# The out-projection of a hybrid layer in halves of 512 columns, and the step that frees the next input's memory by itself

## The chip, the cores and the metric

The kernel runs on 1 core of a Trainium2 chip. The metric is the device time of one execution in microseconds (us). The engines are named as in the profile: PE (TensorE matmuls) with PEld (its weight loads), DVE (VectorE), ACT (ScalarE), POOL (GpSimd) and SP (SyncE, which issues the DMAs here).

## What is computed

Two layers of a mixer on 1024 latent tokens and 256 context tokens of width 1024, in float32. Each layer normalises its input, modulates it, and projects it at once to the inputs of three branches: a convolution, windowed attention (8 heads, windows of 128 tokens, with the context as extra keys) and a gated linear attention (GLA). Every branch is gated; the three lie side by side as 1024 columns and go through one out-projection, whose result is scaled by a gate and added to the input:

```python
y_l = jnp.concatenate([a_l, b_l, c_l], axis=-1) @ w_out      # [1024, 1024] @ [1024, 1024]
xl = xl + gate[:, None] * y_l
if update_ctx:                                               # first layer alone
    y_c = jnp.concatenate([a_c, b_c, c_c], axis=-1) @ w_out  # [256, 1024] @ [1024, 1024]
    xc = xc + mod_c[2 * D:] * y_c
...
return _rms_norm(xl) * final_norm_w
```

## The kernel before

Tokens are worked in 10 tiles of 128: tiles 0 and 1 are the context, 2 to 9 the latent tokens. The second layer needs no out-projection of the context, so there are 10 + 8 = 18 tiles to project out. All matrix products are made in three passes: each operand is split into hi + lo (a cast to the narrower type `F32R`, and the difference), and `three` (L670) adds hi x hi, hi x lo and lo x hi over 8 k-tiles of 128 rows.

*What sets the order.* The program is written as generators ("lanes"). Each yields conditions (a buffer is free, a flag is set, a tile is written). `loop` (L201) runs them against a small model of the engines' clocks at build time: of the lanes whose condition holds, the one with the lowest priority number issues its next instructions. The engines then run their instructions strictly in that order. The model counts a matmul of 256 columns as 107 ns and one of 512 as 213 ns, so a change in one lane can move instructions of all others. Out-projection tiles have priority 8 and more, the in-projection and the layer's main lane (`program`, `phase_a`, `phase_bc`) 9, attention 1 to 2.

*Memory.* WS0 and WS1 hold one group of 256 weight columns each, hi and lo (4096 columns a partition). WR0 to WR2 hold raw pieces from memory (512 columns). SM0 to SM14 are small tiles. H1, H2_0, H2_1 and HC hold the modulated input as hi and lo; attention and the out-projection reuse them later: HC for keys and queries, H1 for values, probabilities and the hi half of a token tile. In the profile the numbers of buffers are left out: H is H1, H2_0 or H2_1, ps a PSUM bank.

*The in-projection's end and attention.* The last two groups of the in-projection (6 and 7, attention's gates) take turns by token chunks, and attention starts among them. Group 6 gives back its WS slot after its last chunk, group 7 after its own, which is the last of all; the flag `h2out` then says that H2_0 and H2_1 are free.

*The out-projection's weights* are loaded by `loader` (L650) in four quarters of 256 columns: o0 in a WS slot, o1 in H2_0 after `h2out`, o2 in a WS slot, o3 in H2_1. A quarter comes in four pieces of two k-tiles (256 KB, 2 KB a partition), each a DMA to a WR slot and a split: a cast on ACT or DVE and a subtraction on DVE or POOL.

*The out-projection of a tile* (`out_tiles`, L1465) waits for both attention units of the tile, splits the tile's 1024 columns of the mixed branches into hi and lo, and multiplies: the token tile is the stationary side, the weights move. `out_mm` (L1442) does a quarter, 24 matmuls of 256 columns; two quarters fill a PSUM bank of 512 columns. Two lanes take the even and the odd tiles. The last two tiles hold two banks at once and do quarters 0 and 2 first. `x_old` (L1513) loads the old x to a WR slot between two quarters, `out_tail` (L1519) multiplies by the gate, adds the old x, sums the squares and stores the tile for the next layer.

*The end of a layer.* `phase_bc` (L1627) waits for all attention units and for the flags `ml` of both lanes, then frees two pieces of memory and sets `hfree..1` (the next input's tiles 2 to 5 may be written); then it waits for the whole out-projection and sets the flags for the other tiles. It does so in the main lane, of priority 9.

Of the kernel before, what the change touches and what calls it, by code (L numbers as in the profile page):

```python
# [34 lines left out]
class Engine:  # L35
    """an engine whose instructions are also put on the model's clock"""
# [12 lines left out]
class Model:  # L49
    """Estimate of when each engine is free and when each part of a tile was last written and read.  # L50
    It only decides the order in which instructions are issued; what has to wait for what is up to Tile."""
# [9 lines left out]
    def part(self, ap):  # L61
        """the times of ap's tile (written, read, written as seen by PE) and the pieces of it that ap covers"""
# [94 lines left out]
class Lane:  # L157
    """a generator of stages: what it yields says when its next stage may be issued"""
# [6 lines left out]
class Hybrid:  # L165
# [10 lines left out]
    # ---------------------------------------------------------------- issue order  # L176
# [6 lines left out]
    def when(self, c, lane):  # L183
        """the time from which condition c holds, None if that is not known yet"""
# [16 lines left out]
    def loop(self, last):  # L201
        """issues stages until lane `last` is done: of those that may start by now, the first by priority"""
# [33 lines left out]
    # ---------------------------------------------------------------- memory  # L236
    def memory(self):
# [13 lines left out]
        # a PSUM tile is used by one engine at a time, so there is one a bank, but for two of two banks  # L251
# [18 lines left out]
    def choice(self, cls, wide):  # L270
        """the free slots; those for wide tiles are left to these while self.rsv"""
        s = [x for x in self.slots[cls] if x[1] != self.kept]
        if cls == "SM" and (wide or self.rsv):
            s = [x for x in s if (x[1] in self.narrow) != wide]
        return s
# [14 lines left out]
    def mix_new(self, dt):  # L290
        """the upper half of mix anew, to hold what it doesn't hold yet"""
        t, old = self.tile("mix4", 4 * TC, dt), self.mixes[1]
        m, b = self.nc.part(t)
        m[1, b] = self.nc.touched(old) if old is not None else 0.0
        self.mixes[1] = t
        return t

    def mix(self, a, t, p=slice(None)):
        """tokens t of mix a, or of several that lie in the same half of mix"""
# [6 lines left out]
    def bank_of(self, cls, pair):  # L306
        """the bank that class cls would get"""
# [35 lines left out]
    def at(self, ap):  # L343
        """condition: all that has been issued has written ap"""
        return lambda: self.nc.written(ap)

    def rest(self, ap):
        """condition: nothing issued uses ap any more"""
        return lambda: self.nc.touched(ap)

    def sm_spare(self, cols):
        """like sm(), from the spare place if that is free"""
        return self.get("SF")[:, 0:cols] if self.slots["SF"] else self.sm(cols)

    # engines that can do the same work: the one that is done first
    def pick(self, *opts):
        """opts: (engine, estimated cost, function)"""
# [4 lines left out]
    def split(self, hi, lo, src):  # L362
        """hi + lo = src exactly, both float32r; src in SBUF"""
# [6 lines left out]
    def copy(self, o, a):  # L370
        """from PSUM"""
# [11 lines left out]
    def scale(self, o, a, s, f=1.0):  # L383
        """o = a * s * f; s one value a partition"""
# [6 lines left out]
    def square(self, junk, a, o):  # L391
        """o = sum of a * a"""
# [6 lines left out]
    # ---------------------------------------------------------------- set-up  # L399
# [37 lines left out]
    def rope_free(self):  # L437
        """between its uses the memory of the rotary table is one more small tile"""
# [3 lines left out]
    def rope_load(self):  # L442
        """generator: the rotary table again"""
# [24 lines left out]
    # ---------------------------------------------------------------- modulation  # L468
    def mod_add(self, l, b0, mt):
        """blocks b0 .. of the modulation from PSUM [128, blocks, 2], with their bias"""  # L470
# [9 lines left out]
    def mod_group(self, l, b0, n, raw):  # L480
        """generator: n blocks of 128 columns of the modulation, four k-tiles at a time in the column groups of the PE array;
        raw: the k-tiles of w_mod, loaded here if None"""
# [32 lines left out]
    # ---------------------------------------------------------------- h  # L515
    def hslot(self, i):
        """chunk and column offset of token tile i in the T-layout h"""
# [6 lines left out]
    def views(self):  # L524
        """the memory of h, free for it once the first weights have gone through"""
# [14 lines left out]
    def rstd(self, ss, scale, n):  # L540
        """(ss * scale + eps) ** -0.5 on [128, n]"""
# [13 lines left out]
    def part_h(self, l, i, k0, n, x):  # L555
        """generator: k-tiles k0 .. k0 + n - 1 of h for token tile i, from its normalised [128, 128 n] piece x"""
# [36 lines left out]
    def first_x(self, i, xt):  # L593
        """generator: token tile i of the input, loaded to xt and normalised there"""
# [16 lines left out]
    # ---------------------------------------------------------------- weights  # L611
# [14 lines left out]
    def load_w(self, key, src, ap, tile=None):  # L626
        """256 weight columns, split into hi and lo; ap(hl, k): k-tiles k and k + 1"""
        w = self.new_w(key, ap, tile)
        for k in range(0, 8, 2):
            self.go(self.piece(w, src, k), 3)  # L630

# [18 lines left out]
    def loader(self):  # L650
        """generator: all weights in the order of their use"""
# [6 lines left out]
        for l in range(2):  # L658
# [4 lines left out]
            yield from ws((l, "o0"), I["w_out"][l, 0])  # L663
            yield f"h2out{l}"
            self.load_w((l, "o1"), I["w_out"][l, 1], self.ws_ap(self.H2[0]))
            yield from ws((l, "o2"), I["w_out"][l, 2])
            self.load_w((l, "o3"), I["w_out"][l, 3], self.ws_ap(self.H2[1]))

    # ---------------------------------------------------------------- in-projection
    def three(self, out, st, mv, k0, k1):  # L670
        """out += st(hi,lo)^T mv(hi,lo) over k-tiles k0 .. k1 - 1 of 8, three float32r passes"""
# [7 lines left out]
    def t_group(self, l, g, ev, ctx_blocks, order=(1, 2, 0), lat_blocks=(0, 1), after=None, last=True):  # L679
        """T layout: ev(block, psum [128, n], t0, n, chunk)"""  # L680
# [1150 lines left out]
```

## Time and profile before

| | |
|---|---|
| time, median of 3 runs | 1357.74 us (1356.18, 1357.74, 1364.62) |
| span of the profiled execution, first to last instruction | 1357.4 us |
| PE busy | 1268.0 us, 93% of the span |
| PEld busy | 1084.6 us, 80% |
| DVE busy | 951.0 us, 70% |
| ACT busy | 558.6 us, 41% |
| POOL busy | 543.8 us, 40% |
| granted TensorE clock, mean | 0.983 |

The profile shows one execution; its own time is known as its span, 0.3 us under the median of the runs. A row of instructions gives their operation, the tiles written and read, the shape and the count. For a matmul the moving side comes first: `ps<-WS,H` moves weights in WS past a token tile in H. A matmul's duration is its way through the array, and several are under way at a time. Nearly all instructions carry the line of one helper (L43), so they are told apart by their tiles. Windows give busy us of an engine in a stretch, with the instructions' count.

### The profile page before, as it was taken

The page shows a single profiled execution, that of the slowest core. Times are in us where ns is not written, and L with a number is a line of the kernel's source. Part 1 is how long each engine was busy: PE and PEld are TensorE (multiplying, and loading weights), DVE is VectorE, ACT ScalarE, POOL GpSimd, SP SyncE. Part 2 cuts the span into 40 slices and gives each one's busy share as a digit, 9 for nine tenths or more (in the row PEclk, how much of TensorE's full clock was granted, in tenths as well). Part 3 has the DMA queues.
Part 4 walks back from the last instruction along what each step waited for, and adds up shares of the span by engine and source line. Part 5 has one row for each costly group of instructions (what it writes and reads, how often), then busy time and mean ns, then how long its engine had stood idle before and what let it go on. Part 6 is the DMA issues. An engine that isn't in the chain of part 4 may idle for free.

```text
span 1357.4 us, 24183 instructions
## 1 busy us (share of the span) xinstructions
PE 1268.0 (93%) x9070; PEld 1084.6 (80%) x9070; DVE 951.0 (70%) x1852; ACT 558.6 (41%) x1239; POOL 543.8 (40%) x769
## 2 busy tenths in 40 slices
PE   6999986898999999999999989988899999999997
PEld 3667976787788676887998978977797888898997
DVE  5844895789655366875666686896957478887864
ACT  3720351121223364665663451251113156776751
POOL 1410046766222233464353032046783244645530
PEclk9999997899999999999999999989999999999999
DMA  9353112321212433343113452113322113311112
GB/s 331 137 147 97 55 32 58 83 79 44 67 32 65 131 118 89 104 129 97 42 55 98 132 191 62 55 37 78 97 57 77 34 48 101 98 44 51 62 37 78
DMA packets 105045, 116.46 MB, mean 86 GB/s; under 512 B 38464, under 2 KB 65376, under 8 KB 104928
## 3 DMA queue, kind: packets, MB, share of 16 engines
q1 hardware_dynamic: 104928, 114.92, 28.4%
q8 instruction: 71, 1.16, 0.3%
q14 instruction: 46, 0.38, 0.1%
HBM read 95.47 MB, written 19.42 MB: 85 GB/s over the span
## 4 chain that ended last, share of the span: by engine, by line
PE 49%; DVE 10%; POOL 8%; issue 5%; DMA 4%; ACT 2%; SPq 0%; POOLq 0%; DVEq 0%; ACTq 0%
PE ps L43 49%; DVE SM L43 5%; POOL SM L43 5%; DVE H L43 2%; DMA WR<-in_w_in_dram 2%; POOL WR L43 2%; DVE WS L43 1%; DVE mix L43 1%; ACT SM L43 1%; POOL tir L43 1%; DMA SM<-kd 0%; DMA SM<-x 0%; SPq L43 0%; DMA WR<-in_w_out_dram 0%; DMA x<-SM 0%
## 5 line engine op out<-in xcount | busy, mean ns | idle before, releaser
L43 PE MATMUL ps<-H,WS 128*128 128x512 f32 x1344 | 339.2, 400 | 4.2 <-DVE stat L43 2.4
L43 PEld LDWEIGHTS ps<-H,WS 128*128 128x128 f32 x1344 | 245.6, 189 | 71.4 <-issue 17.6
L43 ACT ACTIVATE SM<-ps 128x512 f32<-128x512 f32 (+4 forms) x172 | 91.0, 533 | 427.0 <-PE ps L43 353.5
L43 PE MATMUL ps<-WS,H 128*128 128x256 f32 x1704 | 254.0, 291 | 6.3 <-DVE SM L43 3.7
L43 PEld LDWEIGHTS ps<-WS,H 128*128 128x128 f32 x1704 | 229.2, 195 | 21.9 <-issue 11.6
L43 PE MATMUL ps<-idr,SM 128*128 128x128 f32 (+1 forms) x1076 | 150.1, 272 | 34.6 <-POOL SM L43 27.8
L43 DVE SCALAR_TENSOR_TENSOR mix<-U,small,mix 128x1295 f32<-128x1295 f32 (+1 forms) x120 | 176.6, 1517 | 0.2
L43 PEld LDWEIGHTS ps<-idr,SM 128*128 128x128 f32 (+1 forms) x1076 | 122.8, 142 | 58.3 <-POOL SM L43 32.9
L43 DVE SCALAR_TENSOR_TENSOR H<-ps,H 128x512 fp32r<-128x512 f32 x160 | 106.2, 683 | 59.7 <-ACT H L43 59.6
L43 POOL TENSOR_TENSOR SM<-SM,SM 128x256 f32<-128x256 f32 (+4 forms) x89 | 70.5, 799 | 179.8 <-ACT SM L43 142.6
L43 ACT ACTIVATE H<-ps 128x512 fp32r<-128x512 f32 x176 | 99.6, 597 | 86.7 <-PE ps L43 81.6
L43 POOL TENSOR_TENSOR tir<-tir,mhalf 128x1 f32<-128x1 f32 (+2 forms) x55 | 44.4, 810 | 205.3 <-DVE tir L43 177.8
L43 ACT ACTIVATE SM<-SM,stat 128x641 f32<-128x641 f32 (+2 forms) x144 | 110.4, 768 | 34.9 <-DVE stat L43 27.1
L43 DVE CUSTOM_DVE_ANT_0 SM<-ps,SM,small 128x640 f32<-128x640 f32 (+2 forms) x128 | 101.9, 808 | 18.8 <-PE ps L43 18.5
L43 PE MATMUL ps<-H 128*128 128x512 f32 x320 | 99.3, 412 | 2.0 <-DVE H L43 1.8
L43 PE MATMUL ps<-H,H 128*128 128x256 f32 x552 | 98.2, 286 | 0.0
L43 POOL TENSOR_TENSOR SM<-SM,WR 128x128 f32<-128x128 f32 (+2 forms) x113 | 88.5, 801 | 13.1 <-DVE SM L43 9.3
L43 PE MATMUL ps<-SM,SM 128*32 128x128 f32 (+4 forms) x764 | 80.3, 291 | 13.4 <-DVE SM L43 8.8
L43 POOL TENSOR_SCALAR SM<-SM,tir 128x640 f32<-128x640 f32 (+2 forms) x86 | 73.5, 869 | 38.5 <-DVE tir L43 30.4
L43 PEld LDWEIGHTS ps<-H,H 128*128 128x128 f32 x552 | 82.3, 189 | 4.7 <-issue 3.4
L43 PE MATMUL ps<-WS,SM 128*128 128x256 f32 x248 | 69.4, 280 | 0.0
L43 PE MATMUL ps<-H,SM 128*128 128x256 f32 x248 | 69.4, 280 | 0.0
(150 smaller groups left out, 2126.7 us busy)
## 6 DMA issues: line engine op xcount, KB each, us to landing
WR<-in_w_in_dram SPq DMA_DIRECT2D x80, 256.0 KB, 3.9
WR<-in_w_mod_dram SPq DMA_DIRECT2D x64, 256.0 KB, 3.0
WR<-in_w_out_dram SPq DMA_DIRECT2D x32, 256.0 KB, 3.3
SM<-vd SPq DMA_DIRECT2D x116, 64.0 KB, 2.4
x<-SM SPq DMA_DIRECT2D x20, 256.0 KB, 2.5
SM<-x SPq DMA_DIRECT2D x20, 256.0 KB, 4.6
qd<-SM SPq DMA_DIRECT2D x18, 256.0 KB, 2.2
mix<-in_x_dram SPq DMA_DIRECT2D x8, 512.0 KB, 8.0
```

The lines of the kernel that those rows point to most:

```text
L43: r = getattr(self._e, op)(*a, **k)
```

## The change

The out-projection's columns are worked in two halves of 512. A half's weights take two buffers, hi in one and lo in the other: half 0 in both WS slots, half 1 in H2_0 and H2_1. They come in eight rows of one k-tile and 512 columns (`load_o`, `row_of`: 256 KB, two runs of 1 KB a partition). `out_mm` does k-tiles k0 to k1 of a half with matmuls of 512 columns, and the old x is loaded between its two calls. The last two tiles are worked like the others. The two flags `ml` are set once. What followed the wait for attention in `phase_bc` is a lane of its own, `h_free`, of priority 0. Comments are dropped as well.

```diff
+    def load_o(self, l, p, tiles):
+        v = [t.rearrange("p (k c) -> p k c", k=8) for t in tiles]
+        w = self.new_w((l, f"o{p}"), lambda hl, k: v[hl][:, k], tiles)
+        w.one = w.ap
+        for k in range(8):
+            self.go(self.row_of(w, self.I["w_out"][l, 2 * p:2 * p + 2], k), 3)
+    def row_of(self, w, src, k):
+        yield self.need("WR")
+        raw = self.get("WR")
+        self.nc.sync.dma_start(raw.rearrange("p (q c) -> p q c", q=2), src.rearrange("q p (k c) -> p q k c", k=8)[:, :, k])
+        yield
+        self.split(w.ap(0, k), w.ap(1, k), raw)
+        self.free(raw)
+        w.t[k] = self.nc.end
...
-            yield from ws((l, "o0"), I["w_out"][l, 0])
+            t = []
+            for _ in range(2):
+                yield self.need("WS")
+                t.append(self.get("WS", F32R))
+            self.load_o(l, 0, t)
             yield f"h2out{l}"
-            self.load_w((l, "o1"), I["w_out"][l, 1], self.ws_ap(self.H2[0]))
-            yield from ws((l, "o2"), I["w_out"][l, 2])
-            self.load_w((l, "o3"), I["w_out"][l, 3], self.ws_ap(self.H2[1]))
+            self.load_o(l, 1, self.H2)
...
-    def out_mm(self, l, i, y, q):
-        key = (l, f"o{q}")
-        for k in range(0, 8, 2):
-            yield self.w_at(key, k), self.w_at(key, k + 1)
-            self.three(y[:, q % 2 * 256:(q % 2 + 1) * 256], self.gk[i], self.w[key].one, k, k + 2)
-        self.left[q] -= 1
-        if self.left[q] == 0 and q in (0, 2):
-            self.free(self.w[key].tile)
+    def out_mm(self, l, i, y, p, k0, k1):
+        key = (l, f"o{p}")
+        for k in range(k0, k1):
+            yield self.w_at(key, k)
+            self.three(y, self.gk[i], self.w[key].one, k, k + 1)
+        self.left[p] -= k1 == 8
+        if p == 0 and self.left[p] == 0:
+            self.free(*self.w[key].tile)
...
-            if n < len(blocks) - 2:
-                for p in range(2):
-                    yield None, self.bank_need("ac")
-                    y = self.bank_get("ac")
-                    yield from self.out_mm(l, i, y, 2 * p)
-                    xo = yield from self.x_old(l, i, p)
-                    yield from self.out_mm(l, i, y, 2 * p + 1)
-                    z.append(self.go(self.out_tail(l, i, p, y, xo), 2))
-            else:
...
+            for p in range(2):
+                yield None, self.bank_need("ac")
+                y = self.bank_get("ac")
+                yield from self.out_mm(l, i, y, p, 0, 4)
+                xo = yield from self.x_old(l, i, p)
+                yield from self.out_mm(l, i, y, p, 4, 8)
+                z.append(self.go(self.out_tail(l, i, p, y, xo), 2))
             self.free(*m)
-            if n + 2 >= len(blocks) - 2:
+            if len(blocks) - 4 <= n < len(blocks) - 2:
                 self.flag(f"ml{l}.{par}")
...
+        self.go(self.h_free(l), 0)
+        yield self.outs
+        self.flag(f"hfree{l + 1}0")
+        self.flag(f"hfree{l + 1}2")
+    def h_free(self, l):
         yield tuple(u.lane for u in self.units), f"ml{l}.0", f"ml{l}.1"
         self.slots["SF"] = []
         self.flag(f"hfree{l + 1}1")
         self.free(self.amask)
-        yield self.outs
-        self.flag(f"hfree{l + 1}0")
-        self.flag(f"hfree{l + 1}2")
```

PE's order where the first layer's out-projection begins. Before, in the middle of gate group 7 (HC alone: attention's scores; H1 alone: its values; WR with cst: the modulation of the second layer):

```order
L43 MATMUL ps4_70<-H1_6_111 128x512 x2
L43 MATMUL ps5_71<-WS0_596_4620,H1_6_111 128x256 x6
L43 MATMUL ps4_70<-H1_6_111 128x512 x2
L43 MATMUL ps1_67<-HC_103_490 128x256 x2
L43 MATMUL ps1_67<-HC_103_490 128x384 x2
L43 MATMUL ps2_68<-WR0_620_4722,cst_89 32x512
L43 MATMUL ps2_68<-WR2_623_4741,cst_89 32x512
L43 MATMUL ps5_71<-WS0_596_4620,H1_6_111 128x256 x6
```

The same place with the change, from group 7's last block (WS1_404) on:

```order
L43 MATMUL ps1_67<-H2_1_105_492,WS1_404_3772 128x512 x6
L43 MATMUL ps3_69<-idr_81,SM8_600_4637 128x128
L43 MATMUL ps3_69<-idr_81,SM3_601_4638 128x128
L43 MATMUL ps3_69<-idr_81,SM2_602_4639 128x128
L43 MATMUL ps3_69<-idr_81,SM1_603_4640 128x128
L43 MATMUL ps2_68<-H1_6_111 128x512 x2
L43 MATMUL ps4_70<-sel_90,SM9_641_4859 128x2 x4
L43 MATMUL ps5_71<-WS0_596_4620,H1_6_111 128x512
L43 MATMUL ps5_71<-WS1_645_4878,H1_6_111 128x512
L43 MATMUL ps5_71<-WS0_596_4620,H1_6_111 128x512
```

The first out-projection matmul stands behind group 7's last block now; its three passes read hi in WS0, lo in WS1 and hi again.

SP's order at the out-projection's first loads, before:

```order
L43 DMA U_63<-qd_105 128x512
L43 DMA WR2_601_4621<-in_w_out_dram 128x512
L43 DMA WR1_602_4625<-in_w_out_dram 128x512
L43 DMA WR0_603_4629<-in_w_out_dram 128x512
L43 DMA WR2_611_4657<-in_w_out_dram 128x512
L43 DMA WR0_617_4700<-in_w_mod_dram 128x512
L43 DMA WR1_618_4702<-in_w_mod_dram 128x512
```

And with the change:

```order
L43 DMA WR2_627_4769<-in_w_mod_dram 128x512
L43 DMA WR1_628_4772<-in_w_mod_dram 128x512
L43 DMA U_63<-kd_106 128x128
L43 DMA SM13_630_4777<-kd_106 128x128
L43 DMA WR0_663_4879<-in_w_out_dram 128x2x256
L43 DMA WR2_664_4883<-in_w_out_dram 128x2x256
L43 DMA WR1_665_4887<-in_w_out_dram 128x2x256
```

The first weights moved behind eight loads of the modulation's weights and two small loads of attention's keys and values (kd).

PE's order at the end of the first layer, the last out-projection matmuls and the second layer's first group, before:

```order
L43 MATMUL ps2_68<-H2_1_105_492,SM1_1016_7255 128x256
L43 MATMUL ps2_68<-H2_1_105_492,HC_103_490 128x256 x2
L43 MATMUL ps2_68<-H2_1_105_492,SM1_1016_7255 128x256
L43 MATMUL ps0_66<-H1_6_111,WS0_1035_7453 128x512 x24
L43 MATMUL ps3_69<-idr_81,SM9_1058_7570 128x128 x4
```

And with the change:

```order
L43 MATMUL ps2_68<-H2_0_104_491,HC_103_490 128x512
L43 MATMUL ps2_68<-H2_1_105_492,HC_103_490 128x512
L43 MATMUL ps2_68<-H2_0_104_491,SM8_1024_6929 128x512
L43 MATMUL ps0_66<-H1_6_111,WS1_1035_7022 128x512 x24
L43 MATMUL ps4_70<-idr_81,SM11_1055_7083 128x128 x4
```

The border itself stands as before: 24 matmuls of the second layer's group 0, then transposes of its input (idr with SM).

More of the change, by code (lines that the diff above doesn't have):

```diff
@@ L1458, in out_proj @@
     def out_proj(self, l, blocks):
-        self.left = [len(blocks)] * 4
+        self.left = [len(blocks)] * 2
         lanes = [None, None]
@@ L1488, in out_tiles @@
             z = []
-            if n < len(blocks) - 2:
-                for p in range(2):
-                    yield None, self.bank_need("ac")
-                    y = self.bank_get("ac")
-                    yield from self.out_mm(l, i, y, 2 * p)
-                    xo = yield from self.x_old(l, i, p)
-                    yield from self.out_mm(l, i, y, 2 * p + 1)
-                    z.append(self.go(self.out_tail(l, i, p, y, xo), 2))
-            else:
-                y, xo = [], []
-                for p in range(2):
-                    yield None, self.bank_need("ac")
-                    y.append(self.bank_get("ac"))
-                    yield from self.out_mm(l, i, y[p], 2 * p)
-                for p in range(2):
-                    xo = yield from self.x_old(l, i, p)
-                    yield from self.out_mm(l, i, y[p], 2 * p + 1)
-                    z.append(self.go(self.out_tail(l, i, p, y[p], xo), 2))
+            for p in range(2):
[5 more added lines that the diff above has]
+                z.append(self.go(self.out_tail(l, i, p, y, xo), 2))
             self.free(*m)
-            if n + 2 >= len(blocks) - 2:
+            if len(blocks) - 4 <= n < len(blocks) - 2:
                 self.flag(f"ml{l}.{par}")
```

## Prediction

> **What bounds the kernel now.** I read the engines' busy shares first, then the busy time by stage, then PE's waits in the stages that the change touches.
>
> ```profile
> span 1357.4 us, 24183 instructions
> PE 1268.0 (93%) x9070; PEld 1084.6 (80%) x9070; DVE 951.0 (70%) x1852; ACT 558.6 (41%) x1239; POOL 543.8 (40%) x769
> ...
> 510.00:782.00 272.00, 263.38 (x1873) 229.56 (x1872) 187.25 (x408) 149.45 (x333) 107.68 (x176) 0.99 0.32 94
> 782.00:1157.00 375.00, 355.47 (x2503) 306.47 (x2503) 281.53 (x513) 128.85 (x284) 166.64 (x226) 0.98 0.26 75
> 1157.00:1350.00 193.00, 185.42 (x1416) 174.01 (x1414) 146.32 (x295) 117.13 (x252) 85.55 (x130) 1.00 0.20 62
> ```
>
> PE is busy 93% of the span. The out-projection runs beside attention from 510 to 782 us (first layer) and from 1157 to 1350 us (second). PE is idle there for only 272.00 - 263.38 = 8.6 us and 193.00 - 185.42 = 7.6 us, at granted clocks of 0.99 and 1.00. So these stages last as long as PE's own stream, and the question is what one matmul costs in that stream. The longest single waits of PE that the change could touch are these two, in the list of instructions by time (the bracket is the idle time ahead and its releaser):
>
> ```profile
> 738.83 0.36 PE L43 MATMUL ps<-WS,H 128*128 128x256 f32 x1 [2.51 <-DVE SM L43]
> ...
> 790.30 1.32 PE L43 MATMUL ps<-idr,SM 128*128 128x128 f32 x8 [2.85 <-ACT SM L43]
> ```
>
> The first is an out-projection matmul that waits for its token tile's lo half, the second a transpose of the second layer's input.
>
> **The change part by part.** *Half as many matmuls, each twice as wide.* A token tile takes 96 matmuls of 256 columns now (4 quarters, 8 k-tiles, 3 passes) and 48 of 512 afterwards. The groups give these durations:
>
> ```profile
> L43 PE MATMUL ps<-H,WS 128*128 128x512 f32 x1344 | 339.2, 400 | 4.2 <-DVE stat L43 2.4 <-ACT U L43 1.7
> L43 PE MATMUL ps<-H,SM 128*128 128x256 f32 x248 | 69.4, 280 | 0.0
> ...
> L43 PEld LDWEIGHTS ps<-H,SM 128*128 128x128 f32 x248 | 46.9, 189 | 0.0
> ```
>
> The mean of one matmul (280 and 400 ns) is its life in the pipeline, not its price, since the next one starts before it ends. The price is the distance between starts, and the trace has both widths in undisturbed runs:
>
> ```profile
> 770.52 0.40 PE L43 MATMUL ps<-WS,HC 128*128 128x256 f32 x2
> ...
> 781.83 5.63 PE L43 MATMUL ps<-H,WS 128*128 128x512 f32 x24
> ...
> 812.82 24.77 PE L43 MATMUL ps<-H,WS 128*128 128x512 f32 x108
> 837.43 8.16 PE L43 MATMUL ps<-mix,H 128*128 128x288 f32 x60
> ```
>
> From 770.52 to 781.83 us PE does nothing but the last token tile's 96 matmuls: 11.31 us, 117.8 ns each. From 812.82 to 837.43 us it does 108 matmuls of 512 columns: 24.61 us, 227.9 ns each. A tile of 48 wide ones is 48 x 0.2279 = 10.94 us, 0.37 us less. There are 10 + 8 = 18 tiles: **6.7 us less PE work**. The removed 864 weight loads are in this already: one lasts 189 ns, and 117.8 ns is the pace with them, so they lie beside the streaming. I take the whole 6.7 us, because PE is the engine that is last in these stages; below it the gain could be nothing, where another engine sets the pace.
>
> The Trainium skill, "TensorE: Matmul & The Clock Gate", section "Back-to-back issue gap", gives N/2.4 + 2.5 ns between warm matmuls, thus 109.2 and 215.8 ns: an estimate from that page is 10.48 us against 10.36 us a tile, and only 2.2 us over 18 tiles. The trace does not agree with either figure (117.8 and 227.9 ns), and I go by the trace.
>
> *The weights come by rows of two quarters, and the first half needs both WS slots.* Now the first quarter needs the slot of gate group 6 alone. Afterwards hi lies in one slot and lo in the other, which group 7 holds until its last block. What PE did in the meantime, in the first layer:
>
> ```profile
> 526.38 0.88 PE L43 MATMUL ps<-WS,H 128*128 128x256 f32 x6
> ...
> 529.23 0.96 PE L43 MATMUL ps<-WS,H 128*128 128x256 f32 x6
> ...
> 531.10 0.51 PE L43 MATMUL ps<-WS,H 128*128 128x256 f32 x2
> ...
> 532.62 0.75 PE L43 MATMUL ps<-HC 128*128 128x256 f32 x4
> ...
> 546.88 1.64 PE L43 MATMUL ps<-H,WS 128*128 128x512 f32 x6
> ```
>
> Ahead of group 7's last block (546.88) stand 24 out-projection matmuls (6, 6 and the 12 between 531.10 and 532.62), 24 x 0.1178 = 2.8 us of filler, which now comes later. If attention then leaves PE idle for as long, that is 2.8 us lost; if PE goes on with attention's own work, nothing. The second layer:
>
> ```profile
> 1155.81 1.55 PE L43 MATMUL ps<-H,WS 128*128 128x512 f32 x6
> ...
> 1157.78 1.59 PE L43 MATMUL ps<-WS,H 128*128 128x256 f32 x12
> ...
> 1162.51 0.75 PE L43 MATMUL ps<-HC 128*128 128x256 f32 x4
> ```
>
> There the first out-projection matmuls follow group 7 within 2 us, 12 at once and 12 more by 1162.51: again 2.8 us. I take the middle, 1.4 us each, **2.8 us back**.
>
> The new wait itself: the first lo half is a subtraction into WS1, which waits on its engine for group 7's last matmul; behind it on DVE stand the next cast, that block's own gate (which waits for the same matmuls) and the softmax's first step, for which ACT and then PE wait.
>
> ```profile
> L43 DVE TENSOR_TENSOR WS<-WR,WS x65: 677/693/1791, 96.6 to 1167.2; 128x512 fp32r<-128x512 f32 x65
> ...
> L43 DVE CAST WS<-WR x52: 408/427/1554, 96.1 to 1165.2; 128x512 fp32r<-128x512 f32 x52
> ...
> 500.00:550.00 50.00, 48.93 (x257) 35.91 (x256) 32.57 (x60) 23.75 (x48) 16.26 (x22) 0.97 0.34 102
> 550.00:600.00 50.00, 47.76 (x361) 42.77 (x359) 45.79 (x93) 35.78 (x76) 31.85 (x44) 1.00 0.41 119
> 1150.00:1200.00 50.00, 47.44 (x346) 43.61 (x345) 43.13 (x87) 34.75 (x75) 33.25 (x47) 1.00 0.30 87
> ```
>
> A piece costs 0.43 + 0.69 = 1.12 us where DVE does both parts. There are 16 pieces a layer as before, of the same size; but four that lay before 550 us move past it, 4.5 us of DVE work at most, into a stretch where DVE is free for 50.00 - 45.79 = 4.2 us. I take nothing for it; its other end is the slow rival below.
>
> *The loads.* 32 DMAs of 256 KB stay 32, with runs of 1 KB a partition in place of 2 KB, in an order that now has them behind the modulation's loads and two small loads of keys and values on SP.
>
> ```profile
> WR<-in_w_out_dram SPq DMA_DIRECT2D x32, 256.0 KB, 3.3
> ...
> mix<-in_x_dram SPq DMA_DIRECT2D x8, 512.0 KB, 8.0
> ...
> H<-in_w_mod_dram SPq DMA_DIRECT2D x8, 512.0 KB, 9.3
> ```
>
> No row shows this form. The nearest pair is two loads of 512 KB at the start: 9.3 us with 1 KB runs against 8.0 us with 4 KB runs, 16% more; 3.3 us would be 3.8 us. With three WR slots the 16 loads go in about 5 rounds, so a layer could lose 5 x 0.5 = 2.5 us, or nothing. I take nothing: the raw tiles are fetched while group 7 still runs.
>
> *The end of the first layer.* Now WS0 is free 8.5 us before PE's last out-projection matmul (three quarters of 2.8 us behind it), afterwards both slots 24 x 0.228 = 5.5 us before it. The next layer's first weights:
>
> ```profile
> 775.22 0.43 DVE L43 CAST WS<-WR 128x512 fp32r<-128x512 f32 x1 [1.57 <-DMA WR<-in_w_in_dram]
> 775.69 0.69 DVE L43 TENSOR_TENSOR WS<-WR,WS 128x512 fp32r<-128x512 f32 x1
> ```
>
> The first piece is ready at 776.4 us and used at 781.83 us: 5.4 us of cover for 3 us of delay. Nothing, and 3 us if the cover is gone. The freeing step with its own priority may let the second layer's transposes in earlier; PE's rows at the border stand in the same order, so I take nothing here, with -2.85 us (the wait at 790.30) as the other end. In the tail after the last matmul the same operations remain.
>
> **The sum**: -6.7 + 2.8 = -3.9 us against the profiled execution's 1357.4 us span, which stands 0.3 us under the median of 1357.74 us: **1353.5 us**.
>
> **The rivals.** *DVE and the missing filler (slower).* At the start of each out-projection DVE gets all 16 pieces at once. It decides if DVE's 4.2 us of slack from 550 to 600 us is used up; then both the 4.5 us of splits and the 2.8 us of filler are lost, in both layers: -6.7 + 2 x 7.3 = +7.9, 1365.3 us. For it: DVE is at 92% in that stretch. Against: casts may go to ACT and subtractions to POOL, with 14 and 18 us free there.
>
> *The waits at the border go (faster).* The two waits of 2.51 and 2.85 us vanish and the start costs nothing: 1357.4 - 6.7 - 5.4 = 1345.3 us. For it: the flag is no longer set by the lane of lowest priority. Against: both releasers are data of the token tiles, which the flag doesn't make.
>
> *Weight loads set the pace (much faster).* If a matmul cost its mean, a tile would go from 96 x 0.280 = 26.9 to 48 x 0.400 = 19.2 us, 18 x 7.7 = 138 us less, 1219 us. Against it stand the 11.31 us that 96 really take. The same section of that page has 131 ns for a 512-column matmul in a stream with weight loads, an estimate of 6.3 us a tile; the 108 in a row at 227.9 ns speak against it.
>
> *Nothing comes of it.* Attention's chain through DVE, ACT and POOL sets the pace and PE waits longer: 1357.4 us.
>
> **How the numbers follow.** Forecast 0.53 (1349 to 1357 us), slow rival 0.18, fast rival 0.18, nothing 0.09, weight loads 0.02. 1% is 13.6 us, about what a measurement tells from no change, so faster means below 1344.2 us and slower above 1371.3 us. The order of all later instructions is laid anew, and 8.6 + 7.6 us of idle PE can shift either way: that puts half of the fast rival (0.09) and a third of the slow one (0.06) beyond the bound, and 0.03 and 0.01 of the forecast. Faster 0.09 + 0.02 + 0.03 = 0.14, slower 0.07, same the other 0.79. The range takes in both rivals' times and the loads' 2.5 us a layer: 1338 to 1368 us.
>
> **What the profile after would show.** Groups of 512-column matmuls with SM as the stationary side and none of 256; 864 fewer matmuls, PE's busy time less by some 5 to 8 us and PEld's by 864 x 0.189 = 163 us at most, with hardly any effect on the time. A tile alone should last 10.9 us. The first out-projection matmul should come behind group 7's last block, with at most 3 us of new idle time ahead of it. I am wrong if wide matmuls in this loop run at other than 0.228 us, if DVE's busy share at the start reaches 98%, or if PE's idle time in the two stages changes by over 8 us.

## The result, and the profile after

The changed kernel takes **1366.46 us** (median of 6 runs, 1364.89 to 1373.31); the kernel before took 1357.98 us beside it. The ratio is 1.0064, with a 95% interval of 1.0040 to 1.0087: slower by 0.6%, where 1353.5 us, 0.3% faster, had been forecast. The time lies in the forecast range, but it moved the other way.

The page of the changed kernel begins with its span and the engines' busy times:

```profile
span 1364.2 us, 22483 instructions
PE 1267.5 (93%) x8206; PEld 1041.3 (76%) x8206; DVE 963.8 (71%) x1846; ACT 558.1 (41%) x1247; POOL 543.8 (40%) x767
```

The 864 matmuls are gone (9070 to 8206), and PEld is 43 us less busy. PE's busy time is down by 0.5 us only, and DVE's is up by 12.8 us. The stages tell where. Bounds, span of the stage, and busy time of PE, PEld, DVE, ACT and POOL stand in these rows; the bounds are the first matmul of the second layer, the last matmul of its group 7, and PE's last. First the changed kernel, from its first layer's attention on:

```profile
510.00:779.50 269.50, 260.16 (x1400) 204.78 (x1399) 190.97 (x399) 150.54 (x340) 111.25 (x177) 0.99 0.29 92
779.50:1153.70 374.20, 354.47 (x2507) 306.81 (x2506) 280.87 (x508) 129.38 (x287) 165.61 (x225) 0.99 0.26 75
1153.70:1356.40 202.70, 186.44 (x1028) 154.07 (x1026) 154.81 (x299) 115.66 (x250) 82.59 (x128) 0.98 0.20 64
```

Then the last stage of the kernel before, with the same bounds in its trace:

```profile
1157.00:1349.20 192.20, 185.42 (x1416) 174.01 (x1414) 145.59 (x293) 117.13 (x252) 85.55 (x130) 1.00 0.20 63
```

The first two stages did not lose: the second layer begins 2.3 us earlier (779.5 against 781.8 us), and the in-projection keeps its length (374.2 against 375.2 us). The whole loss is the second layer's attention: **202.7 against 192.2 us**. PE's idle time there goes from 192.20 - 185.42 = 6.8 us to 202.70 - 186.44 = 16.3 us. The list of PE's waits in that stage (releaser, sum, times, longest), before:

```profile
PE ps L43 <- DVE SM L43: 1.6, 2, 1.2
PE ps L43 <- POOL SM L43: 1.6, 4, 0.4
PE ps L43 <- DVE stat L43: 1.6, 4, 0.6
PE ps L43 <- DVE H L43: 1.4, 3, 0.8
```

and after:

```profile
PE ps L43 <- DVE H L43: 10.3, 11, 2.4
PE ps L43 <- DVE SM L43: 3.9, 3, 1.9
PE ps L43 <- POOL WS L43: 1.0, 1, 1.0
```

PE waits for DVE, for the lo halves of the probabilities (H) and for their scaling (SM). POOL's WS is the wait for the first lo half of the weights: 1.0 us, once.

### The profile page after: what moved, and what is told of

Read it like the earlier page. It is cut to its first block, busy times and chain, and to the rows that moved or that the text cites. A ratio compares the mean times of both kernels' runs of the same rounds, so it can differ in the third digit from the quotient of the medians.

```text
span 1364.2 us, 22483 instructions
## 1 busy us (share of the span) xinstructions
PE 1267.5 (93%) x8206; PEld 1041.3 (76%) x8206; DVE 963.8 (71%) x1846; ACT 558.1 (41%) x1247; POOL 543.8 (40%) x767
## 5 line engine op out<-in xcount | busy, mean ns | idle before, releaser
L43 PE MATMUL ps<-WS,H 128*128 128x256 f32 (+1 forms) x1428 | 244.2, 316 | 3.0 <-DVE H L43 1.2
L43 PEld LDWEIGHTS ps<-WS,H 128*128 128x128 f32 x1428 | 197.0, 198 | 22.5 <-issue 8.4
L43 PEld LDWEIGHTS ps<-idr,SM 128*128 128x128 f32 (+1 forms) x1076 | 126.3, 144 | 78.4 <-POOL SM L43 32.4
L43 PE MATMUL ps<-H,H 128*128 128x512 f32 x276 | 85.7, 401 | 5.0 <-DVE H L43 3.8
L43 POOL TENSOR_SCALAR SM<-SM,tir 128x640 f32<-128x640 f32 (+2 forms) x77 | 64.6, 851 | 43.3 <-DVE tir L43 37.7
L43 PEld LDWEIGHTS ps<-SM,SM 128*64 128x64 f32 (+2 forms) x764 | 45.6, 128 | 27.3 <-issue 12.7
L43 PEld LDWEIGHTS ps<-H 128*128 128x128 f32 x320 | 55.8, 190 | 13.8 <-DVE H L43 4.4
L43 DVE TENSOR_TENSOR SM<-SM,mix 32x128 f32<-32x128 f32 x144 | 59.6, 414 | 5.4 <-ACT SM L43 3.3
```

What stands on the lines that cost most here:

```text
L43: r = getattr(self._e, op)(*a, **k)
```

## The experiments

Two measures serve throughout: the ratio to the kernel before on the same chip, and the stages of the trace. **Stage A** runs from PE's 2601st matmul (by operation, tiles and shape the order of PE's matmuls is the same in all kernels up to there, and differs first at the 3212th or later) to the first convolution matmul of the second layer: the first layer's attention, and the border. **Stage B** is the second layer's attention, with the bounds above. The table gives the stages of one profiled execution each. Stages are the better measure of a profile: ahead of the 2601st matmul, where nothing differs, the profiles took between 388.4 and 397.5 us, so that two spans compare badly. One program's stage A repeats within 3 us and its stage B within 2 us.

| kernel | ratio (95%) | stage A | stage B |
|---|---|---|---|
| before | 1 | 444.1 | 192.2 |
| after | 1.0064 (1.0040 to 1.0087) | 442.0 | 202.7 |
| freeing step alone | 1.0048 (1.0030 to 1.0065) | 447.7 | 192.8 |
| halves alone | 1.0033 (1.0017 to 1.0049) | 442.6 | 202.9 |
| step, halves in layer 1 of 2 only | 0.9991 (0.9975 to 1.0008) | 443.0 | 191.9 |
| step, halves in layer 2 of 2 only | 1.0112 (1.0090 to 1.0134) | 450.1 | 203.1 |
| quarters, late load | 1.0030 (1.0012 to 1.0048) | 439.3 | 203.2 |
| step, halves by k-tiles | 0.9989 (0.9974 to 1.0004) | 442.1 | 190.5 |
| the same, once more | 0.9978 (0.9964 to 0.9991) | 442.1 | 190.7 |
| the same, narrow matmuls | 0.9998 (0.9985 to 1.0011) | 445.8 | 192.2 |
| narrow once more | 0.9993 (0.9974 to 1.0012) | 445.3 | 191.8 |
| halves by k-tiles, no step | 1.0041 (1.0020 to 1.0063) | 450.6 | 190.4 |
| late quarters, then by k-tiles, no step | 0.9972 (0.9952 to 0.9992) | 442.2 | 192.3 |
| before, another plan | 1.0127 (1.0102 to 1.0151) | 452.3 | (its group 7 ends elsewhere) |
| before, out-projection held back | 1.0088 (1.0068 to 1.0107) | 445.5 | 205.4 |
| before, more DVE work | 1.0075 (1.0055 to 1.0094) | 444.0 | 204.2 |
| before, stage B planned with 360 | 1.0050 (1.0026 to 1.0074) | 446.1 | 200.6 |
| before, stage B planned with 390 | 1.0057 (1.0037 to 1.0077) | 444.5 | 199.9 |
| halves alone, 360 | 1.0064 (1.0040 to 1.0088) | 441.4 | 204.1 |
| halves alone, 390 | 1.0021 (1.0000 to 1.0042) | 441.8 | 199.4 |

My first theory was that the halves start late in the second layer and PE lacks filler, that is, out-projection matmuls to do while attention's chain runs on the other engines.

### Taking the change apart

*The freeing step alone.*

```
+        self.go(self.h_free(l), 0)
-        yield tuple(u.lane for u in self.units), f"ml{l}.0", f"ml{l}.1"
-        self.slots["SF"] = []
-        self.flag(f"hfree{l + 1}1")
-        self.free(self.amask)
         yield self.outs
```

> The kernel before with the freeing step in a lane of its own, quarters as they were. Late-start theory (the change loses because in the second layer the first half's weights need both WS slots, so that the out-projection gives no filler in the first 40 us of attention): no part of the loss is here, 1356 to 1360 us, ratio 0.998 to 1.002. Freeing-step rival (the step of top priority upsets the order): 1362 us or more, at least half of the 8.5 us lost.

Measured 1364.28 us, so the step alone costs 0.5%: the first theory had nothing for it. Stage B is untouched; stage A lost 3.6 us, at the border: from the second layer's first matmul to its first convolution matmul it took 59.9 us instead of 55.6. PE's first transposes of the second layer's input wait there for 6.51 us, where they waited for 2.85 us before:

```profile
794.69 1.97 PE L43 MATMUL ps<-idr,SM 128*128 128x128 f32 x8 [6.51 <-ACT SM L43]
```

SP's queue shows what moved. The kernel before issues weights (WR) between the stores of tiles (x<-SM), and then the loads of the input (SM<-x):

```profile
770.69 0.32 SPq L43 DMA_DIRECT2D x<-SM  x1
771.10 0.87 SPq L43 DMA_DIRECT2D WR<-in_w_in_dram  x2
...
782.99 1.07 SPq L43 DMA_DIRECT2D WR<-in_w_in_dram  x2
784.17 4.82 SPq L43 DMA_DIRECT2D SM<-x  x8
```

With the step alone two stores stand ahead of the first weights, and everything behind them is about 4.7 us later. Of this, 2.8 us lie ahead of the 2601st matmul (396.1 against 393.3 us), where the programs are alike; some 2 us are left for the step:

```profile
773.00 2.71 SPq L43 DMA_DIRECT2D x<-SM  x2
775.76 1.40 SPq L43 DMA_DIRECT2D WR<-in_w_in_dram  x3
...
787.58 1.39 SPq L43 DMA_DIRECT2D WR<-in_w_in_dram  x2
789.02 4.08 SPq L43 DMA_DIRECT2D SM<-x  x8
```

Counted from the 2601st matmul the transposes come 1.6 us later; the rest of their longer wait is that PE gets there sooner.

*Halves alone* (the changed kernel without the step, the same lines the other way round).

> The changed kernel without its freeing step (halves alone, the flags set where they were before). Two-cause theory (the freeing step lengthens the wait at the border of the layers by 2 to 4 us, the late start costs 10 us in the second layer's attention): the wait ahead of the second layer's first transposes falls from 4.49 us to 3 us or less, 1362 to 1365 us, ratio 1.003 to 1.005. Rival that the step costs only beside quarters: 1366 us, as the whole change.

Measured 1364.38 us, ratio 1.0033, as the first of the two expected. By the ratios the step costs 0.3% beside halves too, though the intervals overlap; by stage A, 442.6 against 442.0 us, nothing. The border's first wait is 3.12 us here and 4.49 us with the step, close to the 3 us expected. Of these 1.4 us, 0.6 are left at the first convolution matmul (56.1 against 56.7 us from the border), and the part ahead of the border took 1.2 us longer here, less than the spread. Stage B is 202.9 us without the step, so that the larger loss belongs to the halves.

*Halves in one layer only*, the step in both, quarters as before in the other; the same switch stands in `out_tiles`.

```
+            if l in (0,):
...
+                self.load_o(l, 0, t)
...
+            else:
+                yield from ws((l, "o0"), I["w_out"][l, 0])
...
```

> The changed kernel with quarters in the second layer, halves in the first layer alone. Late-start theory: the first layer's gain alone is left, 1352 to 1356 us, ratio about 0.997. DVE rival (the bunched splits cost in both layers alike): 1361 to 1363 us. Order rival (any newly laid order of attention may be 5 to 10 us better or worse, wherever the halves are): the second layer's stage moves by over 3 us against the kernel before, in either direction.

> The changed kernel with quarters in the first layer, halves in the second layer alone. Late-start theory: the whole loss and none of the gain, 1366 to 1370 us, ratio about 1.008, and PE again waits 8 us or more for DVE's H in the last stage. DVE rival: 1361 to 1363 us. Order rival: not to be foreseen, 1352 to 1370 us.

Measured 1355.53 us (0.9991) and 1373.01 us (1.0112). The stages add up: halves in the first layer have stage A of the changed kernel and stage B of the one before (443.0 and 191.9 us); halves in the second have stage B of the changed kernel (203.1 us) and a stage A near that of the step alone (450.1 against 447.7 us). The DVE rival of equal loss in both layers is out. The second kernel lost more than expected, since beside quarters the step's cost of stage A comes on top.

### Starting earlier, and starting later

*By k-tiles:* the first half's k-tiles 0 to 3, hi and lo, go into the first WS slot, so that it need not wait for the second.

```
-        w = self.new_w((l, f"o{p}"), lambda hl, k: v[hl][:, k], tiles)
...
+            w.ap = w.one = lambda hl, k: w.v[k // 4][:, hl, k % 4]
```

> The changed kernel, but k-tiles 0 to 3 of a half (hi and lo) lie in the first WS slot and k-tiles 4 to 7 in the second, and likewise in the two H2 tiles, so that the first half can start when one slot is free. Late-start theory: the filler is back, 1349 to 1356 us, ratio 0.994 to 0.999. DVE rival (what counts is 16 pieces for the first half): 1360 to 1366 us, since as many pieces are split. Rival that the handling of the last two token tiles costs it: stays at 1364 to 1368 us.

Measured 1356.18 us, 0.9989: the wide matmuls are kept, and the loss is gone. Its last stage:

```profile
1157.50:1347.90 190.40, 183.31 (x1032) 153.19 (x1030) 146.11 (x294) 116.46 (x251) 85.85 (x130) 1.00 0.19 63
```

*Late quarters:* the kernel before with the first quarter held back.

```
+            yield f"h2out{l}"
             yield from ws((l, "o0"), I["w_out"][l, 0])
-            yield f"h2out{l}"
```

> The kernel before (quarters of 256, no freeing step) with the first quarter's load held back until group 7 has done its last block, as the halves have to. Late-start theory: the second layer's attention lengthens from 192 us to 197 to 202 us and PE waits more for DVE's H, 1362 to 1368 us, ratio 1.003 to 1.008. Rival that it is the 16 bunched pieces or the wide matmuls themselves: 1356 to 1360 us, since here only 8 pieces stand ahead of the first quarter.

Measured 1363.84 us. Stage B is 203.2 us with matmuls of 256 columns: the loss needs neither the width nor the 16 pieces. Both runs spoke for a late start; but in stage A the late quarters were the fastest of all, and in these runs the start and the order of attention's instructions changed together.

*Both suspected costs undone:* by k-tiles and without the step.

> Halves by k-tiles (the first half starts in one slot) and without the freeing step: both suspected costs undone, the wide matmuls kept. Two-cause theory: 1349 to 1353 us, ratio 0.994 to 0.997, faster than both kernels. Rival that wide matmuls bring nothing: 1356 to 1359 us.

Measured 1365.87 us, 1.0041, a clear miss. Stage B stays at 190.4 us as it should, but stage A takes 450.6 us. The step that cost 3.6 us beside quarters gains 8.5 us here. In this order PE's queue holds transposes of the second layer's input ahead of the second layer's first matmuls, and stands:

```profile
782.81 0.91 PE L43 MATMUL ps<-idr,SM 128*128 128x128 f32 x4 [3.98 <-DVE SM L43]
...
791.28 2.82 PE L43 MATMUL ps<-idr,SM 128*128 128x128 f32 x12 [6.06 <-ACT SM L43]
793.75 2.91 PE L43 MATMUL ps<-H,WS 128*128 128x512 f32 x6
```

*Another plan for the same work:* the kernel before with one number of the planner's model changed.

```
-            near, far = (200, 200) if e == "pe" else (150, 370)
+            near, far = (200, 200) if e == "pe" else (150, 380)
```

> The kernel before with one number of the planner's model changed (a result counts as written 380 ns after its instruction, not 370): no work is changed, but from the first layer's attention on the order is laid anew. Late-start theory: the time stays within 3 us, 1355 to 1361 us. Order rival (an order is luck, whatever the cause): 5 us or more to either side.

Measured **1376.66 us**, 17 us slower, the largest loss of the study. It settles that an order alone can cost more than the change did.

*Holding the out-projection back, and loading DVE,* each in the second layer alone (one `busy` does two additions of 512 columns on DVE):

```
-        yield
+        yield (lambda: self.fl["h2out1"] + 9000 if "h2out1" in self.fl else None) if l else None
```

```
+            if l:
+                for _ in range(4):
+                    self.go(self.busy(), 3)
```

> The kernel before with one thing changed: in the second layer the out-projection's lanes are held back by 9 us of the plan behind group 7's last block. The weights are loaded and split as early as before. Missing-filler theory (what costs 10 us is that PE has no out-projection work in the first 16 us of attention): the second layer's attention lengthens from 192 us to 198 us or more, 1363 to 1369 us, ratio 1.004 to 1.008. DVE rival (it is the splits that stand behind group 7): they are early here, so 1356 to 1360 us.

> The kernel before with useless work: behind group 7 of the second layer DVE does eight additions of 512 columns more (8 x 0.69 = 5.5 us), at the priority of the weights' pieces; the out-projection starts as early as before. DVE rival: most of the 5.5 us comes out at the end, 1361 to 1364 us, ratio 1.003 to 1.005. Missing-filler theory: PE has its out-projection work in the meantime, at most 2 us lost, 1357 to 1360 us.

Measured 1370.55 and 1368.77 us. Each was to be harmless by one of the theories, and each lost 10 us or more, with stage B at 205.4 and 204.2 us. The added 5.5 us of DVE work are less than half of the 12 us that stage B grew by with them. Nor was "no out-projection work in the first 16 us" right as a reading of the changed kernel: its first out-projection matmul comes 3.9 us behind group 7's last, and eight more from 1159.10 us on.

```profile
1152.57 1.55 PE L43 MATMUL ps<-H,WS 128*128 128x512 f32 x6
...
1157.59 0.50 PE L43 MATMUL ps<-WS,H 128*128 128x512 f32 x1
1159.10 2.11 PE L43 MATMUL ps<-WS,H 128*128 128x512 f32 x8 [1.00 <-POOL WS L43]
```

So the first theory can't be the whole account, and I put a second beside it: what costs is any order of stage B other than the one before.

### Only the order of the last stage

The planner's number (`far`, 370 until then) changes behind group 7 of the second layer and nowhere else:

```
+                        if l and c == 2:
+                            self.nc.far = 360
```

> The kernel before; behind group 7 of the second layer the planner's model counts a result as written 360 ns after its instruction instead of 370. Nothing else changes, and all is alike up to that point. Late-start theory: the out-projection starts as early as before, so that the stage behind group 7 stays at 190 to 195 us, 1355 to 1361 us. Order rival (the order of the kernel before happens to fit the chip, and any other one of this stage loses): 200 us or more for the stage, 1365 us or more.

> As the run before it, with 390 ns. Late-start theory: the stage at 190 to 195 us, 1355 to 1361 us. Order rival: 200 us or more, 1365 us or more.

> The halves without the freeing step, with the model's 360 ns behind group 7 of the second layer. Late-start theory: the stage stays at 200 to 205 us whatever the order, 1362 to 1367 us. Order rival: it spreads as that of the quarters does, so that one of the two orders tried may come under 197 us, 1358 us or less.

> As the run before it, with 390 ns. Late-start theory: 200 to 205 us, 1362 to 1367 us. Order rival: under 197 us in one of the two.

Measured 1366.04 and 1366.33 us for the quarters, 1368.48 and 1362.34 us for the halves. The quarters, with the start as early as ever, take 200.6 and 199.9 us:

```profile
1162.90:1363.50 200.60, 190.64 (x1416) 178.64 (x1414) 150.95 (x299) 115.86 (x249) 81.57 (x127) 0.97 0.19 60
```

```profile
1157.10:1357.00 199.90, 187.76 (x1416) 176.27 (x1414) 152.26 (x306) 111.51 (x244) 80.40 (x125) 0.98 0.19 60
```

The order rival came true for the quarters. (The execution profiled with 360 ns took 1373.44 us, 7.4 us above the median, so that its stage is one of the longer ones; by the medians the two lost 6.7 and 7.0 us.) Of the halves neither came under 197 us, which that rival had allowed; 204.1 and 199.4 us are closer to the 200 to 205 us of the late-start theory. The kernels in which PE's other instructions (without the out-projection's matmuls) stand in stage B exactly as before took 190.4 to 192.8 us. Eight other orders took 199.4 to 205.4 us.

Where in the stage the time is lost tells more. With 360 and 390 ns PE's order differs from the one before only from the 587th and the 509th matmul behind group 7's last, 80 and 69 us into the stage. So I cut stage B at 60 us. Before, with the change, and the quarters planned with 360 ns:

```profile
1157.00:1217.00 60.00, 57.44 (x444) 54.00 (x443) 51.62 (x102) 41.76 (x91) 33.77 (x48) 1.00 0.27 80
1217.00:1349.20 132.20, 127.98 (x975) 120.01 (x973) 93.97 (x193) 75.37 (x162) 51.78 (x82) 1.00 0.17 55
```

```profile
1153.70:1213.70 60.00, 52.02 (x306) 42.02 (x305) 52.41 (x95) 43.72 (x92) 31.78 (x42) 1.00 0.29 92
1213.70:1356.40 142.70, 134.42 (x724) 112.06 (x722) 102.40 (x205) 71.93 (x159) 50.81 (x86) 0.98 0.16 53
```

```profile
1162.90:1222.90 60.00, 57.20 (x428) 53.62 (x427) 49.29 (x97) 40.53 (x88) 32.81 (x47) 0.97 0.26 80
1222.90:1363.50 140.60, 133.44 (x990) 125.02 (x989) 101.66 (x203) 75.34 (x162) 48.76 (x80) 0.96 0.16 51
```

In the first 60 us PE is idle for 2.6 us before, 8.0 us with the change and 2.8 us with 360 ns. Every kernel whose out-projection begins late in this stage (leaving out the other plan, whose group 7 ends elsewhere) has 7.7 to 8.5 us there, in four different orders (the halves, the halves planned with 390 ns, the late quarters, the one held back). Those that begin early have 2.5 to 3.1 us, but for 6.0 us with the added DVE work. Behind the first 60 us PE is idle for 4.2 us before, 8.3 us with the change, and 7.2 and 9.0 us where only the order was changed, with 360 and 390 ns, at clocks of 0.96 and 0.98.

So both theories have a share. About 5.4 of the changed kernel's 10.5 us stand where the weights come late. The rest stands further on, where an order alone loses as much. What is not shown: whether another order of the first 60 us, with an early start and no added work, would keep 2.6 us; none was run. Halves by k-tiles keep both the early start and the old order, and lose nothing.

What the old order has is partly to be seen. The planner also chooses the engine for softmax's scaling. In stage B (rows of 1160 to 1350 us) DVE does 7 of those of 640 columns before, and 18 in the changed kernel; POOL does the others, and ACT. Before and after:

```profile
L43 DVE TENSOR_SCALAR SM<-SM,tir 128x640 f32<-128x640 f32 x7 | 6.2, 922 | 0.1
```

```profile
L43 DVE TENSOR_SCALAR SM<-SM,tir 128x640 f32<-128x640 f32 x18 | 15.7, 913 | 0.1
```

The planner's `scale` takes 130 + 640 / 1.92 = 463 ns for one, and the mean is 913 ns. It is a mean of two kinds: in the 20 traces the 46 scalings beside which POOL worked for less than a fifth of the time took 533 to 553 ns, and beside all 284 that took over 1 us POOL worked for two thirds of the time or more. The 9.5 us are about the whole growth of DVE's busy time in the stage (145.59 to 154.81 us). In all eight slow orders DVE is busy for 150.9 us or more (in one of them 5.5 us are the added work), in the fast ones for 145.6 to 147.2 us. That goes with the loss, and the run with added DVE work agrees. It is not shown to be the cause: giving the scalings back to POOL in a slow order was not tried, and the order planned with 360 ns has 7 of them on DVE in its stage B, as many as before, and loses 8 us all the same.

### The width by itself

```
-            self.three(y, self.gk[i], self.w[key].one, k, k + 1)
+            for c in ((slice(0, 512),) if first or last else (slice(0, 256), slice(256, 512))):
+                m.tensor.matmul(y[:, c], st(a, k), mv(b, k)[:, c], start=first, stop=last)
```

> The halves by k-tiles once more, every instruction of the other engines in the same order, but 22 of the 24 wide matmuls of a half are issued as two of 256 columns each (792 more matmuls and weight loads). This is the width alone. By the two paces (2 x 117.8 against 227.9 ns) 792 x 7.7 ns = 6.1 us more PE work: 1361 to 1364 us, ratio 1.003 to 1.005 against the kernel before, where the wide one had 0.9989. Rival that the width is hidden anyway: within 2 us of the wide one.

> The halves by k-tiles with wide matmuls once more, now on one chip with the narrow form that follows. Width theory: 5 to 7 us below the narrow form. Rival (hidden beside other work): within 2 us of it.

> The halves by k-tiles with 22 of 24 wide matmuls in two of 256 columns, the order of every other engine's instructions the same. Width theory: 792 x 7.7 ns = 6.1 us above the wide form, of which 5 to 7 us show in the medians. Rival: within 2 us of it.

The narrow form takes 22 of 24 wide matmuls in two (the planner counts the two as one wide matmul), and no other engine's order changes. By stages both pairs of profiles agree: stage A is 3.5 us longer narrow (442.1 and 442.1 against 445.8 and 445.3 us), stage B 1.4 us, and from the 2601st matmul to PE's end 4.4 us of the 6.1. The medians on one chip differ by 1.2 us only (1357.45 and 1358.64), as the ratios did on two chips (0.9989 and 0.9998). They were expected 5 to 7 us apart, so this is a miss; with intervals of 1.3 and 1.9 parts in a thousand they hold anything from nothing to some 4 us. That the width gains time rests on the stages.

### A version that beats both

```
+            if l:
+                for h in range(2):
+                    yield self.need("WS")
+                    self.load_o(l, 0, h, self.get("WS", F32R))
...
+            yield f"h2out{l}"
             yield from ws((l, "o0"), I["w_out"][l, 0])
```

> The parts that were best by their stages, put together: the first layer in quarters with the late first load (its attention and border took 439.3 us, the kernel before 444.1), the second layer in halves by k-tiles with the early start (190.4 us of attention, before 192.2), no freeing step. If the stages add up: 1357.4 - 4.8 - 1.8 - 2.1 (in-projection) = 1348.7, so 1347 to 1352 us, ratio 0.992 to 0.996. If the stages depend on one another (each order is luck as a whole): anywhere from 1350 to 1370 us.

Measured 1357.01 us, 0.9972 (0.9952 to 0.9992). 1347 to 1352 us had been expected if the stages add up, so that is a miss. It and the halves by k-tiles (0.9978 and 0.9989) are 0.7 to 0.9% faster than the change. Against the kernel before they are 0.1 to 0.3% faster; one of the three intervals, that of 0.9989, still allows no difference. The stages added up less well than hoped, since stage A of the late quarters repeated 2.9 us longer (442.2), and stage B of the halves by k-tiles 1.6 to 1.9 us longer (192.3).

## Why the prediction was wrong

- **The width gained, but less than 6.7 us.** In the changed kernel's end PE runs 135 wide matmuls alone, from 1325.00 to 1356.03 us, 231.5 ns each; 227.9 ns was taken, from another loop. The gain is a small difference of two large numbers: 48 x 0.2315 = 11.11 us against 11.31 us is 0.20 us a tile, 3.6 us for all 18. The stages gave 4.4 us where the order was kept (of 6.1 us for 792 of the 864 matmuls).
- **"2.8 us back" for the lost filler is the term that failed.** It was bounded by 2.8 us a layer. In the first layer no loss shows: stage A gained 2.1 us (442.0 against 444.1), where the width alone brings 3.5 us, and the rest is within the spread. In the second the stage grew by 10.5 us. PE was idle for 9.5 us more, 5.4 of them in the first 60 us. It was busy for 3.1 us longer than with the halves by k-tiles (186.44 against 183.31 us), about what a slower clock cost (up to 3.4 us, below). The width took 2.1 us off (183.31 against 185.42 us). The bound priced the filler, 24 matmuls that come later, at the time they take on PE, and not what the planner does when they do: it lays the whole stage anew. The prediction said so, but gave it no term in the sum, only a share of the chances; another plan of unchanged work moved the time by 17 us.
- **DVE at nothing** was wrong in the second layer, and not by the splits: in the first 60 us DVE spends 10.7 us on them with the change and 10.5 us before. The scalings of 640 columns and fewer grew there from 2.9 to 6.8 us. The first lo half of the second layer's weights, which the prediction put on DVE, was made by POOL, and PE waited 1.0 us for it. DVE's share at the start reached 96% (19.28 of 20 us), short of the 98% named, where it had been 92% (18.40). The second 20 us before, and the first and second with the change:

```profile
1177.00:1197.00 20.00, 19.55 (x155) 18.48 (x154) 18.40 (x35) 14.23 (x33) 14.69 (x23) 1.00 0.23 69
...
1153.70:1173.70 20.00, 16.52 (x87) 12.24 (x86) 18.20 (x31) 14.36 (x30) 9.77 (x11) 1.00 0.33 103
1173.70:1193.70 20.00, 17.61 (x122) 15.46 (x121) 19.28 (x35) 15.99 (x35) 13.15 (x20) 1.00 0.38 118
```

- **The slow rival's 1365.3 us** nearly is the time, but by luck: its sum has 7.3 us in each layer, and the runs have nothing that shows in the first and 10.5 us in the second. Nor is it more than luck that the time lies in the forecast range, which was made wide for this rival.
- **The border at nothing:** PE's rows stood in the same order, as said, but SP's did not, and the transposes wait for 4.49 us where it was 2.85 us. The step's price changes sign with its company: +3.6 us of stage A beside quarters, about nothing beside halves, -8.5 us by k-tiles.

```profile
789.56 3.71 PE L43 MATMUL ps<-idr,SM 128*128 128x128 f32 x16 [4.49 <-ACT SM L43]
```

- **Loads at nothing** held: the median from issue to landing is 3.4 us with 1 KB runs, against 3.3 us.

```profile
WR<-in_w_out_dram SPq DMA_DIRECT2D x32, 256.0 KB, 3.4
```

- Of the marks named, two told: "PE's idle time in the two stages changes by over 8 us", and wide matmuls at another pace than 0.228 us. PE's busy time fell by 0.5 us instead of 5 to 8. It fell by 3.7 us in stage A and 1.1 us in the in-projection, and rose by 1.0 us in stage B, where matmuls ran at half the clock for a while, and by 3.4 us ahead of the 2601st matmul, where the programs are alike.

## What to carry to other kernels

Where a planner lays the order, a small edit has two effects, the one that it is for and a new order of all that follows, and the second may be the larger: here some 4 us gained by the width, and 10.5 us lost in one stage by a late start and a new order. Measure it by changing a number of the planner that changes no work, before a loss or gain is put down to the edit; and prefer a form of the edit that leaves the order alone, as the halves by k-tiles did. Compare stages that begin where the programs first differ, since the part ahead of them moved by 9 us between profiles of the same instructions.

## What the runs showed of the hardware

Short waits of PE lower its clock when they add up. The kernel before runs stage B at a granted clock of 1.00, and so do those with its order. In the changed kernel PE waits three times for DVE's scalings, 1.89, 1.08 and 0.97 us within 5 us. Behind the first two of these waits the clock is halved, from 1288.0 to 1294.8 us, while matmuls run: one of 512 columns starts 0.43 us behind another (1292.52 and 1292.95). In the 3.41 us ahead PE was busy for 0.71 us:

```profile
1284.58:1287.99 3.41, 0.71 (x3) 1.00 0.00 0
1287.99:1294.82 6.83, 5.50 (x17) 0.50 0.00 0
```

```profile
1286.12 0.30 PE L43 MATMUL ps<-idr,SM 128*128 128x128 f32 x1 [1.89 <-DVE SM L43]
1287.50 0.41 PE L43 MATMUL ps<-idr,SM 128*128 128x128 f32 x2 [1.08 <-DVE SM L43]
1288.88 2.18 PE L43 MATMUL ps<-idr,SM 128*128 128x128 f32 x9 [0.97 <-DVE SM L43]
...
1292.52 0.63 PE L43 MATMUL ps<-WS,SM 128*128 128x512 f32 x1
1292.95 1.91 PE L43 MATMUL ps<-H 128*128 128x512 f32 x4
```

6.8 us at half the clock cost up to 3.4 us, on top of the gaps. In other slow orders a single long wait did it, in rows of 10 us: the quarters planned with 360 ns, where PE waited 4.5 us for DVE, and the halves planned with 390 ns, where it waited 5.2 us.

```profile
1290.00:1300.00 10.00, 5.50 (x28) 4.53 (x27) 8.97 (x16) 4.77 (x11) 5.00 (x6) 0.77 0.01 2
```

```profile
1180.00:1190.00 10.00, 5.26 (x20) 4.30 (x21) 6.59 (x10) 3.89 (x10) 5.08 (x9) 0.66 0.34 104
```

The Trainium skill, "TensorE: Matmul & The Clock Gate", section "What's actually happening", has a clock of one half after an idle window of about 3.4 us. The trace agrees on the half and on the length (6.8 us is two such windows). It differs on the cause: no single gap ahead of 1288 us was longer than 1.9 us, and the window ahead was not idle throughout.

All 20 traces together show where the limit lies. Behind the 2601st matmul the clock was halved 96 times, for 3.41 us or twice that (once four times). In 86 of the cases PE had been busy for 52% or less of the 3.41 us ahead, in ten for 64 to 78%; these ten are not explained. Cut into steps of 3.41 us where the clock's own changes lie, every step at full clock with PE busy for less than 44% had a half clock behind it.
